# Branch 0's merge products in pairs by seven block products, sums and mix on GpSimd, engine orders by slot

## The chip, the core and the metric

One NeuronCore of a Trainium2 chip runs the whole block in one launch. It has five engines with instruction queues of their own: TensorE (PE, matmuls into PSUM; PEld in the profile is its weight load), VectorE (DVE), ScalarE (ACT), GpSimd (POOL) and SyncE (SP, which issues all DMAs here). They run in parallel and wait for each other through semaphores. The metric is the device time of one execution in microseconds, of which the median over several runs counts; a profile shows one execution.

## The reference

A transformer block of width 1024 over 512 tokens (and 16 meta tokens in front): one input projection `proj = rmsnorm(h) @ w_in`, latent attention (branch 0, MLA) and attention with a forget gate (branch 1, FoX), then the merge:

```python
y_mla = (o_mla * jax.nn.silu(z_mla)) @ w_br_mla[l]
...
y_fox = (o_fox * jax.nn.silu(z_fox)) @ w_br_fox[l]
mixed = (jax.nn.sigmoid(gate_a) * y_mla + jax.nn.sigmoid(gate_b) * y_fox) @ w_out[l]
h = h + rmsnorm(mixed, post_norm_g[l])
```

All of it is f32. `gate_a` and `gate_b` are columns of `proj`. The change is in these four lines: the products with `w_br_mla` (1024 x 1024 weights, 512 tokens), the sum of the two gated branches, and the start of the product with `w_out`.

## The kernel before

Every f32 operand of a matmul is split into a high and a low part in a 4-byte matmul format (`wh`, `wl` for weights, `gh`, `gl` for activations): ScalarE casts the high part, VectorE or GpSimd subtracts it from the f32 value (`split_lo`, L104). A product is then three passes, high x high, high x low, low x high. Activations lie transposed, 128 features on the partitions, tokens along the row.

TensorE's order is written out by hand over the whole kernel; on the other engines a scheduler places instructions by priority, and a few are pinned. Weights come by DMA into one of three buffers `wraw` (512 KB each, `wload`, L106), and are split into one of three pairs `wh`/`wl`. Up to the end of the attention, GpSimd makes the low parts of weights; behind it `low[0]` is VectorE, and GpSimd has nothing more to do.

The merge (from L1062):

- A **gate unit** (`gate_unit`, L534; PSUM tile `pg`) computes 128 columns of `gate_a` or `gate_b` from the block's input in 24 matmuls of 512 tokens, and ScalarE puts the tanh of it into a tile `th`. Eleven of the 16 gates fall into the merge.
- **Branch 1** (`pair_py`, L1130) treats the 1024 x 1024 product as a 2 x 2 block matrix of 512, and the tokens as two halves of 256, and forms it by seven block products in place of eight. A pair of output blocks, `i` and `i + 4`, is one unit: seven products of 12 matmuls with 256 tokens, into PSUM tiles `x`, `y`, `z`. For that the weight blocks (`b11`, `b12`, `b21`, `b22`, in `wraw`) are combined by four sums (`comb`, L1128, VectorE) and seven of them are split (`take`, L1141, ScalarE and VectorE); the activation blocks are combined once (`S1` to `S4`). Products shared by several outputs are copied from PSUM by ScalarE (L1171, L1174, L1178), and VectorE adds and multiplies with the gate (`gated`, L1158, two instructions L1160 and L1161).
- **Branch 0** (`py`, L1083) takes the plain way: eight units of 24 matmuls with 512 tokens (PSUM tile `py`), a gate product on VectorE (L1088), the sum with branch 1's result (L1092, VectorE), and the split of the sum for the output product (L1094, L104).
- **The output product** also goes by seven block products, over `wout` blocks held in four tiles `tb0` to `tb3`, which `tsum` (L1097, VectorE) combines, and over sums of the mixed activations that `ssum` (L1104, VectorE) makes; their splits go to `a1`, `a2` and parts of `uTh`, `uTl`.

Of the kernel before, what the change touches and what calls it, by code (L numbers as in the profile page):

```python
# [23 lines left out]
S = 512  # L24
# [31 lines left out]
def block_kernel(ctx: ExitStack, tc: tile.TileContext, x, meta_tokens, pre_norm_g, w_in, fox_forget_b,  # L56
# [474 lines left out]
    gates = [(i, br) for br in (1, 0) for i in PAIRED]  # L531
# [530 lines left out]
    with ExitStack() as mg:  # L1062
# [15 lines left out]
        def halved_g(br):  # L1078
            for k in range(KD):
                nc.scalar.copy(gh[:, k], gT[br][:, k])  # L1080
                split_lo(nc.vector, gl[:, k], gT[br][:, k], gh[:, k])

        def py(i, br):  # L1083
            def get():
                return by_k(wunit([wbr[br][:, :, 128 * i : 128 * i + 128]])[0], KD)

            def done(_, ps):
                nc.vector.scalar_tensor_tensor(out=gT[br][:, i], in0=ths[i, br], scalar=1.0, in1=ps, op0=ALU.add, op1=ALU.mult)  # L1088
            run(unit(f"py{i}{br}", get, lambda k: (gh[:, k, :], gl[:, k, :]), KD, [slice(0, S)], done))
            if br:  # L1090
                return
            nc.vector.tensor_tensor(out=mx[:, i], in0=mx[:, i], in1=gT[1][:, i], op=ALU.add)  # L1092
            src, (h, l) = (mx[:, i, 0:256], [t[:, i] for t in a1]) if i < HK else (mx[:, i], [t[:, i - HK] for t in a2])
            nc.scalar.copy(h, src)  # L1094
            split_lo(nc.vector, l, src, h)

        def tsum(n, half):  # L1097

            ks = slice(2 * half, 2 * half + 2)
            t11, t12, t22, t21 = (t[:, ks] for t in tb)  # L1100
            out, a, b = ((t11, t12, t11), (t12, t22, t12), (t22, t22, t11), (t21, t21, t22))[n]
            nc.vector.tensor_tensor(out=out, in0=a, in1=b, op=ALU.subtract)

        def ssum(ks):  # L1104

            kt = slice(ks.start + HK, ks.stop + HK)
            m11, m21, m12, m22 = mx[:, ks, 0:256], mx[:, ks, 256:512], mx[:, kt, 0:256], mx[:, kt, 256:512]
            for o, p, q, op in ((m22, m21, m22, ALU.add), (m21, m11, m21, ALU.subtract), (m11, m22, m11, ALU.subtract),
                                (m12, m12, m11, ALU.subtract)):
                nc.vector.tensor_tensor(out=o, in0=p, in1=q, op=op)  # L1110
            for x, h, l in zip((m22, m11, m21, m12), sh, sl):
                nc.scalar.copy(h[:, ks], x)
                split_lo(nc.vector, l[:, ks], x, h[:, ks])

        lo_, up = slice(0, 256), slice(256, 512)
        kb = [slice(0, HK), slice(HK, KD)]

        def split_to(to, src):
            nc.scalar.copy(to[0], src)  # L1119
            split_lo(nc.vector, to[1], src, to[0])  # L1120

        A11, A12, A22, S1 = ([t[:, kb[q], ts] for t in (gh, gl)] for q, ts in ((0, lo_), (1, lo_), (1, up), (0, up)))
        S2, S3, S4 = a1, [t[:, :, lo_] for t in a2], [t[:, :, up] for t in a2]

        g11, g21, g12, g22 = (gT[1][:, kb[q], ts] for q, ts in ((0, lo_), (0, up), (1, lo_), (1, up)))

        def comb(out, p, q, op=ALU.subtract):
            nc.vector.tensor_tensor(out=out, in0=p, in1=q, op=op)  # L1128

        def pair_py(i, br):  # L1130

            j, g, wb = i + HK, gT[br], wbr[br]
            ra, rb = (wload([wb[:, :, 128 * f : 128 * f + 128]])[1] for f in (i, j))
            yield
            b11, b21, b12, b22 = ra[:, 0:512], ra[:, 512:], rb[:, 0:512], rb[:, 512:]
            X, Y, Z = (sp.tile([128, 512], F32, tag="s", name=f"{n}{i}{br}")[:, 0:256] for n in "xyz")
            c11, c21, c12, c22 = g[:, i, lo_], g[:, i, up], g[:, j, lo_], g[:, j, up]
            th1, th2 = ths[i, br], ths[j, br]
            room = []

            def take(src):  # L1141
                if not room:
                    uid[0] += 1
                    hl = [wp.tile([128, 1024], F32R, tag=t, name=f"{t}{uid[0]}") for t in ("wh", "wl")]
                    room.extend([[t[:, sl] for t in hl] for sl in (slice(0, 512), slice(512, 1024))])
                to = room.pop(0)
                split_to(to, src)
                return to

            def prod(ps, a, w, first, last):  # L1150
                q = 0
                for k in range(HK):
                    for wx, ax in ((w[0], a[0]), (w[0], a[1]), (w[1], a[0])):
                        mm(ps, wx[:, 128 * k : 128 * k + 128], ax[:, k], start=(first and q == 0), stop=(last and q == 11),
                           skip_group_check=True)
                        q += 1

            def gated(dst, th, ts, ps, add):  # L1158
                if add:
                    held[:] = [nc.vector.tensor_tensor(out=dst, in0=ps, in1=dst, op=ALU.add).ins]  # L1160
                return nc.vector.scalar_tensor_tensor(out=dst, in0=th[:, ts], scalar=1.0, in1=dst if add else ps, op0=ALU.add, op1=ALU.mult)  # L1161

            w11 = take(b11)
            comb(b11, b12, b11)
            t1 = take(b11)
            yield
            comb(b12, b22, b12)
            comb(b11, b22, b11)
            t2 = take(b11)
            prod(X, A11, w11, True, False)  # L1170
            nc.scalar.copy(c11, X)  # L1171
            w21 = take(b21)
            prod(Z, S1, t1, True, False)
            nc.scalar.copy(c22, Z)  # L1174
            t3 = take(b12)
            comb(b21, b21, b11)
            prod(X, S2, t2, False, False)
            nc.scalar.copy(c12, X)  # L1178
            w22 = take(b22)
            prod(Y, A12, w21, True, True)  # L1180
            gated(c11, th1, lo_, Y, True)
            t4 = take(b21)
            prod(X, S3, t3, False, False)
            gated(c22, th2, up, X, True)
            read = held[0]
            prod(Z, S4, w22, False, True)
            gated(c12, th2, lo_, Z, True)
            held[:] = [read]
            prod(X, A22, t4, False, True)
            closed[i] = gated(c21, th1, up, X, False).ins  # L1190

        closed = {}
        pairs = [pair_py(i, 1) for i in range(HK)]
        with tc.issue_after(normed[0]):
            split_to(A11, g11)
            split_to(A22, g22)
            comb(g22, g21, g22, ALU.add)
            split_to(S1, g22)
        run(gate_unit())
        next(pairs[0])  # L1200
        with tc.issue_after(normed[0]):
            comb(g21, g11, g21)
            comb(g11, g22, g11)
            split_to(S2, g11)
        next(pairs[0])
        run(gate_unit())
        with tc.issue_after(normed[0]):
            split_to(A12, g12)
            comb(g12, g12, g11)
            split_to(S3, g21)  # L1210
            split_to(S4, g12)
        for i in range(HK):
            for _ in pairs[i]:
                pass
            for half in range(2):
                run(gate_unit())
                held.clear()
            if i == 0:
                for n, (q, c) in enumerate(((0, 0), (0, 1), (1, 1), (1, 0))):
                    for half in range(2):  # L1220
                        k0 = HK * q + 2 * half
                        nc.sync.dma_start(tb[n][:, 2 * half : 2 * half + 2], wout[:, k0 : k0 + 2, 512 * c : 512 * c + 512])
            with tc.issue_after(closed[i]):
                for n in ((), (0,), (1,), (2, 3))[i]:
                    for half in range(2):
                        tsum(n, half)
        halved_g(0)
        for n, i in enumerate(PAIRED):
            py(i, 0)
            if gates:  # L1230
                run(gate_unit())
            elif n >= 4:
                done = n // 2 if n < 7 else HK
                if n in (4, 5, 7):
                    ssum(slice({4: 0, 5: 2, 7: 3}[n], {4: 2, 5: 3, 7: 4}[n]))

        nc.scalar.activation(eps_t[0:1, 0:1], ths[PAIRED[-1], 0][0:1, 0:1], AF.Square)
        nc.scalar.activation(eps_t[0:1, 0:1], eps_t[0:1, 0:1], AF.Sqrt)


        mgg.close()
# [20 lines left out]
        def put_in(n, c, to):  # L1262
            raw = tb[n][:, 2 * c : 2 * c + 2]
            hi, lo = (t.rearrange("p k s -> p (k s)").rearrange("p (k f) -> p k f", k=2) for t in to)
            nc.scalar.copy(hi, raw)
            split_lo(nc.vector, lo, raw, hi)
# [39 lines left out]
        X, Z = ([op5.tile([128, 512], F32, tag="po", name=f"{n}{r}") for r in range(2)] for n in "xz")  # L1306
        Y = [acc(f"y{r}") for r in range(2)]
        s_ = list(zip(sh, sl))
        product(X, a1, 0, lambda c: plain(0, 0, c), True, False)
        for r in range(2):  # L1310
            nc.scalar.copy(yo[:, r, N0], X[r])
# [82 lines left out]
```

## Time and profile before

| | us |
|---|---|
| median of 3 runs | 587.23 |
| lowest, highest run | 587.06, 587.66 |
| span of the profiled execution (first to last instruction) | 584.6 |
| first matmul of branch 1's pairs | 408.61 |
| first matmul of branch 0's products | 491.56 |
| first matmul of the output product | 540.52 |

The page gives the busy time of each engine and, as "the chain that ended last", what released what, from the last instruction back. A busy engine is not the bound by itself; the chain and the waits tell that. In rows by group, `out<-in` names tiles, then come the shapes (partitions x elements), the count, busy time and mean duration, and idle time ahead with what ended it.

### The profile page before, as it was taken

How to read it: one execution, taken by the hardware profiler on the slowest of the kernel's cores; microseconds unless marked ns; L12 is line 12 of the kernel's file. 1: busy time of each engine (PE TensorE's matmuls, PEld its weight loads, DVE VectorE, ACT ScalarE, POOL GpSimd, SP SyncE). 2: the span in 40 equal slices, each digit the busy share in tenths (PEclk: the TensorE clock that was granted, in tenths of full speed). 3: DMA queues.
4: the chain of work that ended last, by engine and by line, in shares of the span. 5: the costliest groups of instructions: out<-in, count | busy, mean ns of one | idle time of the engine just before them, and what ended most of it. 6: DMA issues, size and time to landing. Idle time of an engine off the chain costs nothing.

```text
span 584.6 us, 11115 instructions
## 1 busy us (share of the span) xinstructions
PE 575.7 (98%) x3841; PEld 496.8 (85%) x3841; DVE 416.4 (71%) x1156; ACT 357.4 (61%) x816; POOL 199.4 (34%) x270
## 2 busy tenths in 40 slices
PE   8999999999999999999999999999999999999996
PEld 6989889889889888888898898878998998888884
DVE  5854877885776775767758748896647876468966
ACT  7856774893774775767748747944343462443762
POOL 4317745464468462654554634510000000000000
PEclk9999999999999999999999999999999999999998
DMA  8535599989977999988986976977722534233503
GB/s 295 122 83 163 127 176 230 231 195 248 177 167 158 228 191 206 219 172 207 183 176 180 219 154 147 183 172 236 233 73 72 145 104 144 78 109 108 217 0 144
DMA packets 220000, 97.47 MB, mean 167 GB/s; under 512 B 131456, under 2 KB 209672, under 8 KB 219944
## 3 DMA queue, kind: packets, MB, share of 16 engines
q1 hardware_dynamic: 219944, 96.77, 70.3%
q8 instruction: 30, 0.49, 0.3%
q14 instruction: 26, 0.21, 0.1%
HBM read 62.36 MB, written 3.97 MB: 113 GB/s over the span
## 4 chain that ended last, share of the span: by engine, by line
PE 96%; ACT 1%; DMA 1%; issue 0%; SPq 0%; DVE 0%; POOL 0%; DVEq 0%; ACTq 0%; POOLq 0%
PE z L98 19%; PE pg L98 15%; PE v L98 9%; PE fk L98 8%; PE st L98 8%; PE fq L98 8%; PE x L98 8%; PE py L98 7%; PE ov L98 5%; PE psm L98 3%; PE y L98 2%; PE mq L98 2%; PE mk L98 1%; PE ppe L98 1%; DMA wsr<-in_w_in_dram 1%; ACT uTh L371 0%
## 5 line engine op out<-in xcount | busy, mean ns | idle before, releaser
L104 POOL TENSOR_TENSOR wl<-wraw,wh 128x1024 fp32r<-128x1024 f32 (+2 forms) x61 | 118.3, 1947 | 112.2 <-ACT wh L131 80.5
L131 ACT CAST wh<-wraw 128x1024 fp32r<-128x1024 f32 (+1 forms) x72 | 74.6, 1042 | 56.4 <-PE py L98 16.8
L826 ACT ACTIVATE sf<-sf,nb 128x272 f32<-128x272 f32 (+3 forms) x128 | 72.7, 569 | 11.5 <-DVE nb L791 10.6
L865 DVE SCALAR_TENSOR_TENSOR pn<-sf,ri,pn 128x512 f16<-128x512 f32 (+3 forms) x128 | 69.6, 609 | 1.6 <-ACT pn L861 1.5
L104 DVE TENSOR_TENSOR wl<-wraw,wh 128x512 fp32r<-128x512 f32 (+1 forms) x55 | 52.2, 950 | 23.9 <-ACT wh L1119 17.8
L861 ACT ACTIVATE pn<-sf,ri 128x128 f16<-128x128 f32 (+3 forms) x128 | 59.7, 548 | 0.5 <-DVE ri L831 0.5
L98 PE MATMUL z<-uTh,wh 128*128 128x512 f32 x128 | 50.9, 398 | 0.0
L98 PE MATMUL pg<-uTh,wh 128*128 128x512 f32 x128 | 50.2, 392 | 0.0
L98 PE MATMUL z<-uTl,wh 128*128 128x512 f32 x128 | 50.1, 391 | 0.0
L98 PE MATMUL z<-uTh,wl 128*128 128x512 f32 x128 | 50.0, 390 | 0.0
L98 PE MATMUL pg<-uTl,wh 128*128 128x512 f32 x128 | 49.9, 390 | 0.0
L98 PE MATMUL pg<-uTh,wl 128*128 128x512 f32 x128 | 49.8, 389 | 0.0
L706 DVE TENSOR_REDUCE vsc<-v 128x1 f32<-128x272 f32 (+1 forms) x32 | 13.2, 433 | 39.8 <-PE v L98 39.8
L98 PE MATMUL st<-hlk,hlq 64*128 64x272 f32 (+4 forms) x480 | 41.3, 299 | 0.0
L1119 ACT CAST wh<-wraw 128x512 fp32r<-128x512 f32 x28 | 17.3, 618 | 37.9 <-DVE wraw L1128 17.0
L98 PE MATMUL v<-uTh,wl 128*128 128x256 f32 (+1 forms) x128 | 36.5, 285 | 0.0
L98 PE MATMUL fk<-uTl,wh 128*128 128x256 f32 (+1 forms) x128 | 36.4, 285 | 0.0
L98 PEld LDWEIGHTS st<-hlk,hlq 64*128 64x128 f32 x480 | 33.0, 186 | 4.1 <-ACT vh L725 2.8
L98 PE MATMUL fk<-uTh,wh 128*128 128x256 f32 (+1 forms) x128 | 36.4, 285 | 0.0
L98 PE MATMUL v<-uTl,wh 128*128 128x256 f32 (+1 forms) x128 | 36.4, 285 | 0.0
L98 PE MATMUL fk<-uTh,wl 128*128 128x256 f32 (+1 forms) x128 | 36.4, 285 | 0.0
L98 PE MATMUL v<-uTh,wh 128*128 128x256 f32 (+1 forms) x128 | 36.4, 284 | 0.0
(295 smaller groups left out, 1612.3 us busy)
## 6 DMA issues: line engine op xcount, KB each, us to landing
wraw<-in_w_in_dram SPq DMA_DIRECT2D x56, 512.0 KB, 4.8
cbp<-c_dram SPq DMA_DIRECT2D x16, 264.0 KB, 4.1
wraw<-in_w_br_fox_dram SPq DMA_DIRECT2D x8, 512.0 KB, 4.5
tb<-in_w_out_dram SPq DMA_DIRECT2D x8, 512.0 KB, 5.4
wraw<-in_w_br_mla_dram SPq DMA_DIRECT2D x8, 512.0 KB, 4.3
wraw<-in_w_out_dram SPq DMA_DIRECT2D x6, 512.0 KB, 3.6
xr<-in_x_dram SPq DMA_DIRECT2D x4, 512.0 KB
out_dram<-yo SPq DMA_DIRECT2D x8, 256.0 KB, 2.0
```

Of the source, the lines that this page charges most:

```text
L98: nc.tensor.matmul(*a, **k)
L104: return eng.tensor_tensor(out=lo, in0=src, in1=f32(hi), op=ALU.subtract)
L131: nc.scalar.copy(wh[:, :n], raw[:, :n])
L706: nc.vector.tensor_reduce(out=sc[:, i : i + 1], in_=ps, op=ALU.max, axis=AX.X, apply_absolute_value=True)
L826: exps[b // 3] = nc.scalar.activation(sf, sf, AF.Exp, bias=sums["nb"][:, h, b : b + 1], scale=-1.0, accum_out=sums["su"][:, h, b : b + 1]).ins
L861: normed[:] = [nc.scalar.activation(hi, sf, AF.Copy, scale=rib).ins]
L865: nc.vector.scalar_tensor_tensor(out=lo, in0=sf, scalar=rib, in1=hi, op0=ALU.mult, op1=ALU.subtract)
L1119: nc.scalar.copy(to[0], src)
```

## The change

Branch 0's weights go by the same pairs of seven block products as branch 1's: `add_pair(i, br)` takes the place of `pair_py` and `py`, for both branches. Weight sums (`tcomb`), most activation sums, `tsum`, `ssum` and the sum of the branches (`mixed`) are put on GpSimd (`EP`). The first split of the mixed activations (`a1`, three of four blocks), most of the `ssum` splits, that of `a2`'s upper half and one half of the last `tb3` split go to GpSimd too, cast and difference. Branch 0's gates come in another order, and gate units stand 1, 1, 1, 2 behind branch 1's pairs and 2, 1, 1, 0 behind branch 0's (before: two behind each branch-1 pair, one behind branch 0's first unit).

The order on ScalarE, VectorE and GpSimd is no longer left to the scheduler: TensorE's work of the merge is a list `slots` (one block product, or a quarter of a gate, each), and `at(n, fn)` notes what the others get just ahead of slot `n`; `play` writes it all out in this order. Loads stand 8 and 6 slots ahead of a pair.

```diff
+        EV, EP = nc.vector, nc.gpsimd
+        def split_to(to, src, eng=None):
+            (eng.tensor_copy if eng else nc.scalar.copy)(to[0], src)
+            return split_lo(eng or nc.vector, to[1], src, to[0]).ins
+        def comb(eng, out, p, op, q):
+            eng.tensor_tensor(out=out, in0=p, in1=q, op=ALU.add if op == "+" else ALU.subtract)
         def tsum(n, half):
...
-            nc.vector.tensor_tensor(out=out, in0=a, in1=b, op=ALU.subtract)
+            comb(EP, out, a, "-", b)
...
+        def at(n, fn, *a):
+            aux.setdefault(n, []).append(lambda: fn(*a))
+        def add_gate():
...
+            at(n - 8, lambda: getattr(st["g"][0][1], "load")())
+            at(n - 2, lambda: st["g"][0][1].prep())
+            for q in range(4):
+                slots.append(lambda q=q: run(st["g"][2 * q : 2 * q + 2]))
+        def add_pair(i, br):
...
+            def mixed(f, ts):
+                if not br:
+                    comb(EP, mx[:, f, ts], mx[:, f, ts], "+", gT[1][:, f, ts])
+            at(n - 8, load, j, "b12", "b22")
+            at(n - 6, load, i, "b11", "b21")
+            at(n - 4, tcomb, "b12", "b22", "-", "b12")
+            at(n - 3, take, "w11", "b11")
+            at(n - 2, tcomb, "b11", "b12", "+", "b11")
+            at(n - 2, take, "w21", "b21")
+            at(n - 1, take, "t2", "b11")
+            at(n - 1, tcomb, "b21", "b21", "-", "b11")
+            at(n, banks)
+            at(n, tcomb, "b11", "b22", "-", "b11")
+            at(n + 1, evict, c11, "X")
+            at(n + 1, take, "t1", "b11")
+            at(n + 2, gated, c11, "t1", lo_, "Y", True)
+            at(n + 2, take, "t3", "b12")
...
+            for ps, a, key, first, last in (("X", A11, "w11", True, False), ("Y", A12, "w21", True, True),
+                                            ("X", S2, "t2", False, False), ("Z", S1, "t1", True, False),
+                                            ("X", S3, "t3", False, False), ("Z", S4, "w22", False, True),
+                                            ("X", A22, "t4", False, True)):
+                slots.append(lambda *p, a=(ps, a, key, first, last): prod(*a))
...
         for i in range(HK):
+            n = add_pair(i, 1)
+            for _ in range((1, 1, 1, 2)[i]):
+                add_gate()
...
+            if i in (1, 2):
+                at(n + (3, 1)[i - 1], tsum, i - 1, 0)
+                at(n + (5, 3)[i - 1], tsum, i - 1, 1)
+            if i == 2:
+                at(n + 5, comb, EP, h21, h21, "+", h22)
...
+        for i in range(HK):
+            n = add_pair(i, 0)
+            for _ in range((2, 1, 1, 0)[i]):
+                add_gate()
+            if i == 0:
+                for q in range(4):
+                    at(n + (1, 3, 5, 8)[q], tsum, 2 + q // 2, q % 2)
...
+        region.enter_context(tc.manual_schedule(engines={mybir.EngineType.Activation, mybir.EngineType.DVE, mybir.EngineType.Pool}))
+        def play(first, last):
+            for n in range(first, last):
...
+                    for fn in aux.get(n, []):
+                        fn()
+                if 0 <= n < len(slots):
+                    slots[n]()
...
+        at(end + 4, early[1], EP)
+        at(end + 5, early2[1], EP)
+        at(end + 5, last[1], EP)
+        for q in (3, 2):
+            for fs in (early, early2, last):
+                at(end + 6, fs[q], EP)
+        at(end + 7, blocks, S4, HK, up, slice(0, HK), EP)
+        at(end + 7, lambda: w4.append(put_in(3, 0, a1)))
```

**First piece: pair 2 of branch 1.** VectorE before, in its whole order: `wraw74` and `wraw75` hold the pair's weight blocks, `wl76` to `wl79` are the low parts that its products read, L1128 are the weight sums, L1102 `tsum`, L1160 and L1161 the gate instructions.

```order
L104 TENSOR_TENSOR wl76_5957<-wraw74_5949,wh76_5956 128x512
L1128 TENSOR_TENSOR wraw74_5949<-wraw75_5951,wraw74_5949 128x512
L1128 TENSOR_TENSOR wraw75_5951<-wraw75_5951 128x512
L104 TENSOR_TENSOR wl76_5957<-wraw74_5949,wh76_5956 128x512
L1128 TENSOR_TENSOR wraw74_5949<-wraw75_5951,wraw74_5949 128x512
L104 TENSOR_TENSOR wl77_5966<-wraw74_5949,wh77_5965 128x512
L1128 TENSOR_TENSOR wraw74_5949<-wraw74_5949 128x512
L104 TENSOR_TENSOR wl77_5966<-wraw74_5949,wh77_5965 128x512
L104 TENSOR_TENSOR wl78_5998<-wraw75_5951,wh78_5997 128x512 x2
L104 TENSOR_TENSOR wl79_6032<-wraw74_5949,wh79_6031 128x512
```

VectorE in the changed kernel at the same place; the pair's low parts are now `wl74`, `wl75`, `wl77` and `wl79`, and L1196 and L1197 are the gate instructions.

```order
L104 TENSOR_TENSOR wl74_5871<-wraw73_5833,wh74_5870 128x512 x2
L104 TENSOR_TENSOR wl75_5890<-wraw73_5833,wh75_5889 128x512 x2
L1196 TENSOR_TENSOR gT1_779<-y21_5905,gT1_779 128x256
L1197 SCALAR_TENSOR_TENSOR gT1_779<-th21_5435,gT1_779 128x256
L104 TENSOR_TENSOR wl77_5939<-wraw71_5795,wh77_5938 128x512 x2
L104 TENSOR_TENSOR wl79_5974<-wraw73_5833,wh79_5973 128x512
```

GpSimd in the changed kernel there (before it had no instruction in the merge): the weight sums (L1087) of `wraw71` and `wraw73`, the two halves of `tb1`, and the first sum of branch 0's activations `gT0`.

```order
L1087 TENSOR_TENSOR wraw73_5833<-wraw71_5795,wraw73_5833 128x512
L1087 TENSOR_TENSOR wraw73_5833<-wraw73_5833 128x512
L1087 TENSOR_TENSOR wraw73_5833<-wraw71_5795,wraw73_5833 128x512
L1087 TENSOR_TENSOR tb1_5462<-tb2_5463,tb1_5462 128x1024 x2
L1087 TENSOR_TENSOR gT0_778<-gT0_778 128x4x256
```

The four weight sums and the two halves of `tb1` have moved from VectorE to GpSimd, one after another there, and a sum of `gT0` is new behind them; the splits have stayed on VectorE, each behind a cast of what GpSimd has summed.

**Second piece: branch 0's first products.** VectorE before, from the first `py`: whole weight tiles are split, a gate product (L1088) and the sum of the branches (L1092) stand between them.

```order
L104 TENSOR_TENSOR wl91_6395<-wraw91_6392,wh91_6394 128x1024
L104 TENSOR_TENSOR wl92_6428<-wraw92_6425,wh92_6427 128x1024
L1088 SCALAR_TENSOR_TENSOR gT0_778<-th00_5744,py000_6363 128x512
L1092 TENSOR_TENSOR gT0_778<-gT0_778,gT1_779 128x512
L104 TENSOR_TENSOR wl93_6463<-wraw93_6460,wh93_6462 128x1024
```

VectorE in the changed kernel, from the activation splits for branch 0's pairs to the last weight split of its first pair.

```order
L104 TENSOR_TENSOR wl89_6240<-wraw88_6213,wh89_6239 128x512
L104 TENSOR_TENSOR a2l_5468<-gT0_778,a2h_5467 128x4x256
L104 TENSOR_TENSOR wl89_6240<-wraw88_6213,wh89_6239 128x512
L104 TENSOR_TENSOR wl90_6261<-wraw88_6213,wh90_6260 128x512
L104 TENSOR_TENSOR gl_5454<-gT0_778,gh_5453 128x4x256
L104 TENSOR_TENSOR wl90_6261<-wraw88_6213,wh90_6260 128x512
L1196 TENSOR_TENSOR gT0_778<-y00_6278,gT0_778 128x256
L1197 SCALAR_TENSOR_TENSOR gT0_778<-th00_5902,gT0_778 128x256
L104 TENSOR_TENSOR wl92_6312<-wraw87_6191,wh92_6311 128x512 x2
L104 TENSOR_TENSOR wl94_6347<-wraw88_6213,wh94_6346 128x512
```

GpSimd there: the weight sums of this pair and the two halves of `tb2`.

```order
L1087 TENSOR_TENSOR wraw87_6191<-wraw87_6191 128x512
L1087 TENSOR_TENSOR wraw88_6213<-wraw87_6191,wraw88_6213 128x512
L1087 TENSOR_TENSOR wraw88_6213<-wraw88_6213 128x512
L1087 TENSOR_TENSOR wraw88_6213<-wraw87_6191,wraw88_6213 128x512
L1087 TENSOR_TENSOR tb2_5463<-tb2_5463,tb0_5461 128x1024 x2
```

Where one whole-tile split stood for each `py`, seven half-tile splits stand for each pair, and behind four of them lies a sum on GpSimd; `tb2` and `tb3` fall into this pair.

**Third piece: the end of GpSimd's order in the changed kernel**, during the output product (casts L1083, differences L104; before, ScalarE and VectorE made all of these).

```order
L1083 CAST uTh_68<-gT1_779 128x256
L104 TENSOR_TENSOR uTl_69<-gT1_779,uTh_68 128x256
L1083 CAST a2h_5467<-gT0_778 128x4x256
L104 TENSOR_TENSOR a2l_5468<-gT0_778,a2h_5467 128x4x256
L1083 CAST a1h_5465<-tb3_5464 128x1024
L104 TENSOR_TENSOR a1l_5466<-tb3_5464,a1h_5465 128x1024
```

The last two rows make half of the weights that the last four blocks of the output product read.

282 lines of the change are left out of this document (153 added, 129 removed).

## Prediction, made before the changed kernel was run

> **What bounds the kernel now.** First the page: busy time by engine, and the chain that ended last.
>
> ```profile
> PE 575.7 (98%) x3841; PEld 496.8 (85%) x3841; DVE 416.4 (71%) x1156; ACT 357.4 (61%) x816; POOL 199.4 (34%) x270
> ...
> PE 96%; ACT 1%; DMA 1%; issue 0%; SPq 0%; DVE 0%; POOL 0%; DVEq 0%; ACTq 0%; POOLq 0%
> ```
>
> TensorE is the bound, and nothing that it waits for stands in the chain. Whatever shortens its work shortens the run, as long as the others still deliver in time. Next the chain in order of time through the merge (start, length, what):
>
> ```profile
> 408.61 1.43 PE x L98 x12
> 410.04 1.44 PE z L98 x12
> 411.48 1.38 PE x L98 x12
> 412.86 1.42 PE y L98 x12
> 414.28 1.38 PE x L98 x12
> 415.66 1.36 PE z L98 x12
> 417.02 1.42 PE x L98 x12
> 418.44 10.91 PE pg L98 x48
> ...
> 491.56 5.44 PE py L98 x24
> 497.00 5.44 PE pg L98 x24
> 502.44 38.08 PE py L98 x168
> 540.52 5.49 PE x L98 x24
> ```
>
> One pair of branch 1 is 9.83 us (the seven rows of 12), two gates are 10.91, a branch-0 unit `py` and a single gate 5.44, an output product 5.44 to 5.49; no row waits. Who works beside it, by stage (length, PE, PEld, DVE, ACT, POOL busy, then the granted clock):
>
> ```profile
> core 0: us, PE busy (x) PEld busy (x) DVE busy (x) ACT busy (x) POOL busy (x), PEclk, DMA share, GB/s
> ...
> 408.40:491.50 83.10, 83.10 (x530) 75.49 (x530) 60.27 (x90) 36.71 (x63) 0.00 (x0) 1.00 0.42 122
> 491.50:540.50 49.00, 49.00 (x218) 40.59 (x217) 30.89 (x46) 19.55 (x30) 0.00 (x0) 1.00 0.39 118
> 540.50:584.60 44.10, 38.31 (x169) 31.22 (x167) 34.33 (x53) 23.98 (x43) 0.00 (x0) 0.96 0.30 120
> ```
>
> GpSimd does nothing at all in the last 176 us; VectorE has slack in each stage. The change fills GpSimd.
>
> **What it saves.** Eight `py` of 5.44 become four pairs of 9.83: 43.5 - 39.3 = **4.2 us** of TensorE. The gates and the output products keep their number. If all else hid, the time would be 587.2 - 4.2 = 583.0.
>
> **What the moved work costs.** Behind row 408 GpSimd gets 97 instructions (15 two-operand ones of 1024 elements, 39 of 512, 30 of 256, one of 768, 12 casts), where it had none. VectorE loses its sums and keeps every split that feeds TensorE. Durations:
>
> ```profile
> L104 POOL TENSOR_TENSOR wl<-wraw,wh 128x256 fp32r<-128x256 f32 x16 | 11.5, 739 | 31.7 <-ACT wh L607 25.8 <-DMA qpe_dram<-gT 5.9
> ...
> L666 POOL TENSOR_TENSOR gT<-gT 128x512 f32<-128x512 f32 x2 | 2.6, 1289 | 2.9 <-DVE gT L659 2.9
> ```
>
> ```profile
> L104 DVE TENSOR_TENSOR wl<-wraw,wh 128x1024 fp32r<-128x1024 f32 x25 | 30.4, 1219 | 6.1 <-ACT wh L131 6.0
> L104 DVE TENSOR_TENSOR wl<-wraw,wh 128x512 fp32r<-128x512 f32 x28 | 19.3, 690 | 17.8 <-ACT wh L1119 17.8
> ...
> L1161 DVE SCALAR_TENSOR_TENSOR gT<-th,gT 128x256 f32<-128x256 f32 x12 | 5.1, 423 | 0.3
> ```
>
> So GpSimd takes 0.74 for 256 and 1.29 for 512 elements, VectorE 0.42, 0.69 and 1.22 for 256, 512 and 1024. Whether the two run side by side, the trace shows at few places. VectorE's rows, then GpSimd's, at the start of the merge and at 93 us:
>
> ```profile
> 379.83 2.35 DVE L104 TENSOR_TENSOR gl<-gT,gh 128x1024 fp32r<-128x1024 f32 x2
> 382.21 3.31 DVE L1128 TENSOR_TENSOR gT<-gT 128x1024 f32<-128x1024 f32 x1
> 385.45 1.21 DVE L104 TENSOR_TENSOR gl<-gT,gh 128x1024 fp32r<-128x1024 f32 x1
> ```
>
> ```profile
> 381.53 2.91 POOL L104 TENSOR_TENSOR wl<-wraw,wh 128x1024 fp32r<-128x1024 f32 x1 [3.36 <-ACT wh L131]
> ```
>
> ```profile
> 93.56 0.68 DVE L104 TENSOR_TENSOR hlq<-fq,hlq 128x512 fp32r<-128x512 f32 x1
> ```
>
> ```profile
> 93.54 2.40 POOL L104 TENSOR_TENSOR wl<-wraw,wh 128x1024 fp32r<-128x1024 f32 x1 [1.65 <-ACT wh L131]
> ```
>
> At 93 us VectorE reads one operand from PSUM (`fq`) and both keep their usual time: 0.68, and 2.40 for GpSimd's 1024. At 382 both of VectorE's operands lie in SBUF, and the two take **turns**. GpSimd's row begins at 381.53, VectorE's second split ends at 382.18, and from there GpSimd needs 2.26, to 384.44. VectorE's sum begins at 382.21, takes 3.31 instead of 1.21 and ends at 385.52, 1.08 behind GpSimd's end. Each waits for the whole of the other's instruction, first come first served, and all that runs beside the other is about 0.14 at an instruction's start.
>
> A rule decides how far that reaches. The Trainium skill has two: "Advanced Engine Details and Errata" (VectorE Performance Modes) names only VectorE's two-port modes as those that block GpSimd; "SBUF — State Buffer" (Who interferes with whom) adds every VectorE instruction with two SBUF inputs against a GpSimd one that reads SBUF. By the first, sums of two f32 operands would not wait and the time would be 583.0; by the second it is the sum below. The 3.31 agrees with the second.
>
> Now the turns by stage. Given are TensorE's time; the instructions on the port by elements; their whole durations (GpSimd 2.40, 1.29, 0.74; VectorE 1.22, 0.69, 0.42); the same with 0.14 off each, the least that turns can take; and the stage laid out.
>
> | stage | PE | GpSimd 1024/512/256 | VectorE 1024/512/256 | whole | held | laid out |
> |---|---|---|---|---|---|---|
> | br. 1 pair 0 + gate | 15.3 | 0/5/0 | 1/8/3 | 14.4 | 12.1 | 15.8 |
> | pair 1 + gate | 15.3 | 2/4/0 | 1/7/3 | 17.3 | 14.8 | 18.1 |
> | pair 2 + gate | 15.3 | 3/4/0 | 1/7/3 | 19.7 | 17.1 | 20.2 |
> | pair 3 + 2 gates | 20.7 | 3/3/0 | 8/7/3 | 26.9 | 23.6 | 25.0 |
> | br. 0 pair 0 + 2 gates | 20.7 | 4/5/4 | 3/7/3 | 28.8 | 25.1 | 29.4 |
> | pair 1 + gate | 15.3 | 0/4/4 | 1/7/3 | 15.4 | 12.7 | 15.3 |
> | pair 2 + gate | 15.3 | 0/8/4 | 1/7/3 | 20.6 | 17.3 | 18.0 |
> | pair 3 | 9.8 | 0/0/6, a cast and a difference of 768 | 1/4/3 | 12.4 | 10.1 | 11.2 |
> | first two output products | 10.9 | 0/4/10 | 4/3/4, one of 768 | 20.0 | 16.5 | 15.2 |
> | the rest | 27.2 | 4/2/8 | 7/11/0 | 29.7 | 25.3 | 32.7 |
>
> A cast on GpSimd counts with its tile size: 0.61 for 512, about 1.1 for 1024.
>
> ```profile
> L668 POOL CAST gT<-pt 128x512 fp32r<-128x512 f32 x2 | 1.2, 610 | 0.0
> ```
>
> "Laid out" means the rows of the four engines in their written order under one another, each beginning when the one ahead on its engine is through, when its data are there and when the port is free. Pair 2 of branch 1 shows how (the order's first piece): GpSimd has its last weight sum, both halves of `tb1` and the 4x256 sum of `gT0` in a row, 1.29 + 3 x 2.40 = 8.5. Between two of them VectorE gets one turn: the last split of `wl75`, a gate product, the first split of `wl77`. The first `wl77` split, which the fifth of the seven products reads, comes through 2.9 instead of 0.69 after it was asked for. TensorE waits 1.0 for `wl75` and 4.0 for `wl77`: 4.9 in this stage. Branch 0's first pair loses 8.7 in the same way (two halves each of `tb2` and `tb3` among its splits; the second piece). At the end the splits of `a2` and of `a1` from `tb3`, last of GpSimd's 12 pairs of cast and difference (third piece), keep the last products waiting 4.6. Laid out with hand-overs left out, the sum moves by less than 2.5.
>
> Over TensorE's time that is 0.5 + 2.8 + 4.9 + 4.3 + 8.7 + 0 + 2.7 + 1.4 + 4.3 + 5.5 = **35.1**. By whole durations it is 40, by held parts 17.0 (where a stage holds less than TensorE's time, 0). I take 35: the orders are strict, and a split that has lost its turn keeps what stands behind it waiting while the port is idle. Laying out the program of before in this way gives the last matmul within 0.3 of its row.
>
> Edits at nothing: ScalarE's evictions and casts (it was busy for 36.71 of 83.10 and 19.55 of 49.00); the weight loads, issued six to eight blocks ahead, over 8 us at 1.4 a block, against
>
> ```profile
> wraw<-in_w_br_mla_dram SPq DMA_DIRECT2D x8, 512.0 KB, 4.3
> ```
>
> and the new order of gates, since each `th` is made before its pair. That VectorE loses its sums gains nothing by itself, since it was not on the chain.
>
> **Sum.** The profiled execution's span is 584.6, 2.6 under the median of 587.2; both have the same work, so I add to the median: 587.2 - 4.2 + 35.1 = 618.
>
> **Rivals.**
> *No turns*: the long row at 382 was a special case, and GpSimd's work hides. Laid out without the port, TensorE waits under half a microsecond in all: **583.0**, faster. For it: GpSimd idle now, VectorE with slack, one such sum row only. Against: three numbers of that place (2.91, 3.31, and 1.08 behind the end) fit turns to a few hundredths. It decides from where GpSimd's rows block for half of what they show: then the 35 falls to 3, less than the 4.2 saved.
> *Turns at their least*: the waits among the stages even out and only held parts count: 587.2 - 4.2 + 17.0 = **600**. Against it: the strict order on three engines.
> *The clock falls*: behind the last matmul TensorE stands idle, and the granted clock follows:
>
> ```profile
> 578.80:581.30 2.50, 0.01 (x1) 0.00 (x0) 1.98 (x5) 0.98 (x3) 0.00 (x0) 1.00 0.55 213
> 581.30:584.60 3.30, 0.00 (x0) 0.00 (x0) 0.48 (x1) 0.00 (x0) 0.00 (x0) 0.51 0.41 159
> ```
>
> 2.5 us of idleness and it is half. Two waits of the layout reach 3 to 4 us (pair 2, the last product). If each has the next 3 us at half speed, 1.5 is lost twice: **621**. The Trainium skill ("TensorE: Matmul & The Clock Gate", What's actually happening) gives windows of about 3.4 us for both ways; by that it would be an estimated 1.7 each.
> *Whole durations in every stage*: 587.2 - 4.2 + 40 = **623**.
> That fewer products run isn't in doubt: the rows of TensorE change from 24 of 512 a unit to 84 of 256 a pair.
>
> **Chances.** Forecast 0.58, clock or whole durations 0.20, least turns 0.13, no turns 0.07, a mix near no change 0.02. Within 0.2% (1.2 us) is what a measurement can't tell from no change: faster 0.07, same 0.02, slower 0.91. The range goes from the least turns to 623 with the clock's loss and a little for GpSimd's spread, 600 to 627; it leaves out 583 and what lies around it.
>
> **What would show it.** GpSimd's 1024 rows above 2.8 and VectorE's 512 splits above 1.2 in pair 2 and in branch 0's first pair, and VectorE's rows with a PSUM operand unchanged at 0.42; TensorE waiting there for `wl` from VectorE, and at the end for `a1l` from GpSimd; a pair without waits at 9.8. Wrong would be: VectorE's splits at 0.69 beside GpSimd's rows (then 583), or TensorE waiting for loads.

## The result, and the profile after

| | before | changed |
|---|---|---|
| median | 587.14 us (4 runs) | 623.45 us (4 runs) |
| lowest, highest | 586.97, 587.66 | 622.63, 624.95 |
| span of the profiled execution | 584.6 | 620.8 |

The changed kernel is slower by a factor of 1.0622 (95% interval 1.0607 to 1.0638), 36.3 us where 31 were forecast. From the page of the changed kernel: busy time of the engines, the clock granted to TensorE by fortieths of the span, and the chain that ended last, by engine.

```profile
PE 587.9 (95%) x3985; PEld 508.9 (82%) x3985; DVE 443.1 (71%) x1136; ACT 362.7 (58%) x833; POOL 348.1 (56%) x367
...
PEclk9999999999999999999999999999989889998997
...
PE 70%; POOL 10%; DVE 8%; ACT 4%; issue 4%; DMA 3%; POOLq 0%; DVEq 0%; ACTq 0%
```

Before, the chain was 96% TensorE, with GpSimd at 0%. Now GpSimd and VectorE hold 18% of it. VectorE has 20 instructions fewer and is busy 26.7 us longer (443.1 against 416.4): its instructions have become longer. What TensorE waits for, by releaser (us in total, times, the longest):

```profile
PE x L98 <- DVE wl L104: 8.4, 6, 3.6
PE z L98 <- DVE wl L104: 5.8, 6, 1.7
PE pg L98 <- DVE wl L104: 3.2, 2, 2.1
PE x L98 <- DVE pad L1378: 3.0, 1, 3.0
PE x L98 <- DVE gT L1196: 2.1, 2, 1.6
```

Pair 2 of branch 1, the first place of the prediction, in the changed kernel's timeline: VectorE, GpSimd, then the matmul that waits (start, length, what). L1087 are the sums now, L1196 and L1197 the gate instructions.

```profile
446.31 2.21 DVE L104 TENSOR_TENSOR wl<-wraw,wh 128x512 fp32r<-128x512 f32 x1 [2.13 <-ACT wh L1083]
448.44 0.41 DVE L1196 TENSOR_TENSOR gT<-y,gT 128x256 f32<-128x256 f32 x1
448.89 2.15 DVE L1197 SCALAR_TENSOR_TENSOR gT<-th,gT 128x256 f32<-128x256 f32 x1
450.97 4.03 DVE L104 TENSOR_TENSOR wl<-wraw,wh 128x512 fp32r<-128x512 f32 x3
```

```profile
445.57 5.19 POOL L1087 TENSOR_TENSOR tb<-tb,tb 128x1024 f32<-128x1024 f32 x2
450.72 2.52 POOL L1087 TENSOR_TENSOR gT<-gT 128x1024 f32<-128x1024 f32 x1
```

```profile
453.85 0.39 PE L98 MATMUL x<-a2h,wl 128*128 128x256 f32 x1 [3.58 <-DVE wl L104]
```

One split of 512 takes 2.21 in place of 0.69, a gate product of 256 takes 2.15 in place of 0.42, and the next split again starts behind a GpSimd sum, the one that begins at 450.72. Between two long rows stands one of 0.41: it reads `y`, which lies in PSUM, and it runs inside the row of GpSimd that lasts until 450.76. TensorE waits 3.58 for the split.

Stage by stage, from the first matmul of each in the timeline of the changed kernel. "Over" is the length less TensorE's own time (15.3, 20.7 and so on, as in the prediction's table; 27.0 in the last row, which ends where its last matmul starts).

| stage | first matmul at | length | over | laid out |
|---|---|---|---|---|
| br. 1 pair 0 + gate | 408.18 | 15.6 | 0.3 | 0.5 |
| pair 1 + gate | 423.79 | 19.0 | 3.7 | 2.8 |
| pair 2 + gate | 442.80 | 22.2 | 6.9 | 4.9 |
| pair 3 + 2 gates | 464.95 | 26.5 | 5.7 | 4.3 |
| br. 0 pair 0 + 2 gates | 491.40 | 28.0 | 7.3 | 8.7 |
| pair 1 + gate | 519.43 | 15.3 | 0.0 | 0.0 |
| pair 2 + gate | 534.73 | 18.4 | 3.1 | 2.7 |
| pair 3 | 553.16 | 11.4 | 1.6 | 1.4 |
| first two output products | 564.59 | 15.1 | 4.2 | 4.3 |
| the rest, to the last matmul at 614.15 | 579.65 | 34.5 | 7.5 | 5.5 |
| sum | | | 40.3 | 35.1 |

40.3 less the 4.2 saved is 36.1, which is the measured difference within 0.2. No stage is off by more than 2.0. The three that exceed their forecast most (pairs 2 and 3 of branch 1 by 2.0 and 1.4, the last row by 2.0) had a granted clock of 0.92, 0.94 and 0.90. But the clock doesn't order the stages by itself: branch 0's first pair (0.94) and the first two output products (0.89) came out below their forecast, and pair 1 of branch 1 is 0.9 above it at full clock. TensorE's rows by windows of the changed kernel (length, busy times, and the granted clock behind POOL's column):

```profile
core 0: us, PE busy (x) PEld busy (x) DVE busy (x) ACT busy (x) POOL busy (x), PEclk, DMA share, GB/s
447.00:456.00 9.00, 4.29 (x29) 3.88 (x29) 8.30 (x7) 2.73 (x5) 6.24 (x3) 0.93 0.03 8
456.00:460.00 4.00, 4.00 (x26) 3.91 (x25) 3.39 (x6) 0.16 (x1) 1.29 (x1) 0.73 1.07 310
485.00:489.50 4.50, 4.50 (x14) 3.55 (x13) 4.50 (x2) 1.56 (x2) 4.06 (x2) 0.62 0.46 117
498.00:504.00 6.00, 4.27 (x23) 3.98 (x24) 5.96 (x6) 2.44 (x5) 5.64 (x4) 0.72 0.00 0
567.00:571.00 4.00, 3.72 (x9) 2.95 (x10) 3.96 (x7) 1.69 (x3) 2.83 (x3) 0.57 0.65 167
605.00:612.00 7.00, 6.12 (x14) 4.46 (x15) 5.21 (x9) 1.64 (x5) 2.02 (x1) 0.52 0.29 112
```

Busy time times the missing share of the clock gives 0.3 + 1.1 + 1.7 + 1.2 + 1.6 + 2.9 = an estimated 8.8 us for the five places (the first two rows are one place). The other 31 or so are waits and the restarts behind them.

### The profile page after: what moved, and what is told of

The parts are those of the page before. It is cut to its first block, busy times and chain, and to the rows that moved or that the text cites. A ratio compares the mean times of both kernels' runs of the same rounds, so it can differ in the third digit from the quotient of the medians.

```text
span 620.8 us, 11543 instructions
## 1 busy us (share of the span) xinstructions
PE 587.9 (95%) x3985; PEld 508.9 (82%) x3985; DVE 443.1 (71%) x1136; ACT 362.7 (58%) x833; POOL 348.1 (56%) x367
## 4 chain that ended last, share of the span: by engine, by line
PE 70%; POOL 10%; DVE 8%; ACT 4%; issue 4%; DMA 3%; POOLq 0%; DVEq 0%; ACTq 0%
PE z L98 16%; PE v L98 8%; PE fk L98 8%; PE pg L98 8%; PE st L98 7%; PE fq L98 7%; DVE wl L104 6%; PE ov L98 5%; POOL wraw L1087 3%; PE x L98 3%; PE psm L98 2%; POOL gT L1087 2%; POOL uTl L104 2%; ACT wh L1083 2%; PE mq L98 2%
## 5 line engine op out<-in xcount | busy, mean ns | idle before, releaser
L104 POOL TENSOR_TENSOR wl<-wraw,wh 128x1024 fp32r<-128x1024 f32 (+2 forms) x61 | 117.7, 1937 | 110.9 <-ACT wh L131 74.3
L104 DVE TENSOR_TENSOR wl<-wraw,wh 128x512 fp32r<-128x512 f32 (+1 forms) x74 | 81.6, 1122 | 51.7 <-ACT wh L1083 45.8
L131 ACT CAST wh<-wraw 128x1024 fp32r<-128x1024 f32 (+1 forms) x63 | 65.1, 1039 | 30.6 <-PE v L98 10.0
L1083 ACT CAST wh<-wraw 128x512 fp32r<-128x512 f32 x56 | 33.3, 620 | 56.9 <-POOL wraw L1087 27.1
```

The costliest lines, as they stand in the source:

```text
L104: return eng.tensor_tensor(out=lo, in0=src, in1=f32(hi), op=ALU.subtract)
L131: nc.scalar.copy(wh[:, :n], raw[:, :n])
L1083: (eng.tensor_copy if eng else nc.scalar.copy)(to[0], src)
```

## The experiments

**GpSimd writes, but reads nothing.** If the turns are the cause, they have to go when GpSimd stays as busy at the same places and only stops reading SBUF. In the changed kernel every GpSimd sum of the merge (and cast and difference of the tail) becomes memsets of about its length:

```diff
+        def blank(out, reads, n):
+            for x in reads:
+                nc.gpsimd.memset(x[tuple(slice(0, 1) if k else slice(None) for k in range(len(x.shape)))], 0.5)
+            for _ in range(n):
+                nc.gpsimd.memset(f32(out), 0.5)
+            half = out.shape[-1] // 2
+            if n == 2 and int(np.prod(out.shape)) > 128 * 256:
+                nc.gpsimd.memset(f32(out[..., :half]), 0.5)
...
         def comb(eng, out, p, op, q):
+            if eng is nc.gpsimd:
+                return blank(out, [p, q], 2)
```

> Each GpSimd sum, cast and difference of the merge is replaced by memsets of the same output tile that take about as long (two whole ones and a half one for 2.40 or 1.29, two for 0.74), and a one-column memset of each input, which keeps the waits on what makes the inputs. GpSimd then writes SBUF but reads none. These sums and splits are left out, so the merge's numbers are others. Turns on reading: no VectorE split waits, the 512 splits of wl stay at 0.69 beside GpSimd's memsets, TensorE's waits fall under 1 us each, and the laid-out orders without the port give 589 (587 to 592). Rival, GpSimd is just slow and stands at a bad place in the order: its rows are as long and stand where they stood, so TensorE waits as before, 615 to 623. Rival, turns on writing too: as slow as the changed kernel, 618 to 624.

Measured: 597.85 us, 1.0173 of before (1.0150 to 1.0195); 25.6 less than the changed kernel, but not 589. The turns are gone: VectorE's splits of 512 in the merge take 689 ns. The waits of TensorE that are left come from the experiment itself, as the next run bears out. GpSimd and TensorE in pair 1 of branch 1:

```profile
427.85 0.10 POOL L1084 MEMSET wraw<- 128x1 f32 x1 [1.40 <-DVE wl L104]
```

```profile
431.67 0.39 PE L98 MATMUL z<-gh,wh 128*128 128x256 f32 x1 [0.76 <-ACT wh L1095]
```

A memset of a column in an input that an earlier split still reads has to wait for that split, here 1.40; a sum only reads the input, as the split does, and needn't wait. So this kernel was run again without these columns for weight sums and `wout` sums:

```diff
-                return blank(out, [p, q], 2)
+                return blank(out, [x for x in (p, q) if x.tensor.name.startswith('gT')], 2)
```

> The first memset kernel waited 10.9 more than the kernel before, at the product with S1 in each pair, and the trace puts it down to my one-column memsets: the one on the shared input of two weight sums had to wait for VectorE's split to have read it, which a sum doesn't. Here those columns are left out for weight sums and wout sums, so that GpSimd's memsets are as long as its sums and wait only for what a sum waits for on its output. Left out are the same sums and tail splits as in the first. Turns on reading, and nothing else: the orders laid out without the port give 583 (582 to 588), faster than before. Rival, part of the loss comes from GpSimd's place and length in the order: it stays near the first, 594 to 600. Rival, the clock: no stretch below 0.95 is left, so nothing there.

Measured: **584.94 us, 0.9967 of before (0.9954 to 0.9980)**. Its page, VectorE's splits of 512 and 1024 in the merge, and GpSimd's memsets of the same tiles as the `tb` sums (two of them and a half one, 0.53, per sum):

```profile
PE 573.4 (99%) x3985; PEld 501.3 (86%) x3985; DVE 392.4 (67%) x1136; ACT 362.9 (62%) x833; POOL 315.2 (54%) x585
```

```profile
L104 DVE TENSOR_TENSOR wl<-wraw,wh 128x512 fp32r<-128x512 f32 x54 | 36.4, 690 | 51.2 <-ACT wh L1095 51.2
L104 DVE TENSOR_TENSOR wl<-wraw,wh 128x1024 fp32r<-128x1024 f32 x14 | 17.1, 1221 | 2.0 <-ACT wh L131 1.9
```

```profile
L1086 POOL MEMSET tb<- 128x1024 f32 x16 | 15.3, 956 | 0.5
```

The same 54 splits in the changed kernel:

```profile
L104 DVE TENSOR_TENSOR wl<-wraw,wh 128x512 fp32r<-128x512 f32 x54 | 55.9, 1060 | 46.0 <-ACT wh L1083 45.8
```

With 54% busy GpSimd, VectorE's rows are back at 690 and 1221 ns, and TensorE's busy time falls by 14.5 (587.9 to 573.4) for the same 3985 matmuls, the slow clock among it. The list of TensorE's waits has 0.2 left in the merge:

```profile
PE z L98 <- DVE wl L104: 0.2, 1, 0.2
```

GpSimd instructions of about the sums' length, in the sums' place in the order, cost nothing as long as they don't read. What they leave out besides the reading is the wait for a weight that a sum reads but doesn't overwrite. The run also bears out that the seven products save time, 2.2 of the 4.2 that were counted.

**The same turns without the change.** Does it need shared tiles, or semaphores between the two engines? The kernel before gets GpSimd work in the merge that nobody waits for, on a scratch tile of its own:

```diff
+        scr = m1.tile([128, 256], BF16, tag="scr", name="scr")
+        nc.gpsimd.memset(scr, 0.0)
+        nc.gpsimd.tensor_copy(scr[:, 0:1], g22[:, 0, 0:1])
+        for n in range(80):
+            nc.gpsimd.tensor_tensor(out=scr, in0=scr, in1=scr, op=ALU.subtract)
```

> The kernel before, with 80 GpSimd instructions added in the merge that nobody waits for: each subtracts a scratch tile of 128x256 bf16 from itself (about 0.74 by the f32 row of that size), from about 397 on. The outputs are not touched. Turns: VectorE's splits that begin beside one are up to 0.6 longer than 0.69 and 1.22, GpSimd's rows up to 1.1 longer, and VectorE's rows with a PSUM operand stay at 0.42. The time stays within 0.5 of before (laid out +0.3), because each turn is short and the splits of this kernel are made well ahead. Rival, no turns for a scratch tile that VectorE never touches (the long rows come from shared tiles or from semaphores): 0.69 and 1.22 unchanged. Rival, every turn costs: 80 turns of about 0.6 on VectorE would bring 10 us or more.

And its counterpart:

```diff
-        for n in range(80):
-            nc.gpsimd.tensor_tensor(out=scr, in0=scr, in1=scr, op=ALU.subtract)
+        for n in range(160):
+            nc.gpsimd.memset(scr, 0.0)
```

> As the kernel with dummy reads, but with 160 memsets of the same 128x256 bf16 tile (0.32 each by the row of that size) in place of the 80 subtractions. Turns on reading: VectorE's splits keep 0.69 and 1.22 and the time stays at 587. Rival, turns on any GpSimd access: splits up to 0.3 longer.

Measured with reads: 589.88, 1.0046 of before (1.0029 to 1.0062); with writes: 586.70, 0.9992 (0.9982 to 1.0002). VectorE by groups between 397 and 480, and GpSimd's group, with reads:

```profile
L104 DVE TENSOR_TENSOR wl<-wraw,wh 128x512 fp32r<-128x512 f32 x26 | 26.7, 1047 | 5.3 <-ACT wh L1119 5.2
...
L1160 DVE TENSOR_TENSOR gT<-y,gT 128x256 f32<-128x256 f32 x3 | 1.3, 425 | 3.0 <-PE y L98 3.0
```

```profile
L1216 POOL TENSOR_TENSOR scr<-scr 128x256 bf16<-128x256 bf16 x80 | 76.0, 950 | 6.3
```

The same, with writes:

```profile
L104 DVE TENSOR_TENSOR wl<-wraw,wh 128x512 fp32r<-128x512 f32 x26 | 17.9, 690 | 17.9 <-ACT wh L1119 17.9
```

```profile
L1216 POOL MEMSET scr<- 128x256 bf16 x160 | 49.9, 312 | 9.2
```

A tile that VectorE never touches makes its splits 1047 long instead of 690, and the row that reads PSUM keeps 425. So it is the reading that takes turns, and neither the data nor a semaphore. It needn't be a sum of two tiles: GpSimd's casts, which read one, take turns too. Two of the same size in the changed kernel, the first beside a split of VectorE, the second beside a row with a PSUM operand:

```profile
594.35 1.39 POOL L1083 CAST uTh<-gT 128x256 fp32r<-128x256 f32 x1
```

```profile
597.37 0.39 POOL L1083 CAST uTh<-gT 128x256 fp32r<-128x256 f32 x1
```

The price of the dummy reads was underrated: 2.8 in place of 0.3. Most of it is one wait, at the end of the stretch, where VectorE had used up its lead (busy for 22.2 of the 22.4 us up to there; with reads):

```profile
PE x L98 <- DVE gT L1160: 2.3, 1, 2.3
```

**Which part costs.** First all of it back on VectorE and ScalarE, in the slot orders of the changed kernel:

```diff
-        EV, EP = nc.vector, nc.gpsimd
+        EV, EP = nc.vector, nc.vector
...
-        at(end + 4, early[1], EP)
+        at(end + 4, early[1])
```

(and so for the other tail splits).

> The changed kernel with its slot orders as they are, but all sums and the mix on VectorE, and the twelve tail splits on ScalarE (cast) and VectorE (difference): GpSimd is idle in the merge again. Turns: no VectorE row of the merge beside a GpSimd one, 512 splits at 0.69; what is left is that VectorE's strict order now holds the sums too, laid out 597 (594 to 600). Rival, the written slot orders are what costs, whichever engine has the sums: 612 or more. Rival, the seven products themselves are slower than counted (84 of 256 take 9.83 only in branch 1): 605 or more, and pairs of branch 0 above 9.83 without a wait.

Then the sums and the mix alone, with the tail splits left on GpSimd:

```diff
-        EV, EP = nc.vector, nc.gpsimd
+        EV, EP, EG = nc.vector, nc.vector, nc.gpsimd
...
-        at(end + 4, early[1], EP)
+        at(end + 4, early[1], EG)
```

> Only the sums and the mix go back to VectorE; the twelve tail pairs of cast and difference (S2 of a1, most of the ssum splits, S4 of a2, half of tb3) stay on GpSimd. Turns, laid out: stages of the pairs without long rows, the tail still held up by GpSimd's casts and differences, 600 (597 to 604). Without turns the same layout gives 590. Rival, the tail is where most of the loss lies: 612 or more.

And the tail splits alone, with the sums left on GpSimd:

```diff
-                at(n + 4, blocks, S2, 0, lo_, slice(0, 3), EP)
+                at(n + 4, blocks, S2, 0, lo_, slice(0, 3))
...
-        at(end + 4, early[1], EP)
+        at(end + 4, early[1])
```

> Only the twelve tail pairs go back to ScalarE and VectorE; the sums and the mix stay on GpSimd. Turns, laid out: the pairs lose what they lost, the tail gains little because the losses ahead of it stay, 617 (613 to 622). Without turns the layout gives 589. Rival, the tail splits on GpSimd are the main loss: 600 or less.

| sums and mix | tail splits | median | of before |
|---|---|---|---|
| GpSimd | GpSimd (the changed kernel) | 623.45 | 1.0622 (1.0607 to 1.0638) |
| GpSimd | VectorE | 623.69 | 1.0620 (1.0601 to 1.0639) |
| VectorE | GpSimd | 602.35 | 1.0249 (1.0223 to 1.0274) |
| VectorE | VectorE | 601.12 | 1.0231 (1.0214 to 1.0249) |

The sums are worth 21 to 23 us, the tail splits nothing that these runs can tell. Both runs with VectorE's splits lie above their forecast and outside its range, 601 against 597 and 624 against 617; the third, 602 against 600, lies within. In the two that miss it, TensorE loses most in one place of the tail: the third output product (`z`) takes 11.8 and 14.4 us from its first matmul to the next product's, in place of 5.44. In the kernel with all on VectorE:

```profile
560.51 0.80 PE L98 MATMUL z<-wh,uTh 128*128 128x512 f32 x1 [2.67 <-ACT wh L131]
561.10 0.63 PE L98 MATMUL z<-wh,uTl 128*128 128x512 f32 x1
564.35 0.79 PE L98 MATMUL z<-wl,uTh 128*128 128x512 f32 x1 [2.62 <-DVE wl L104]
```

Behind two waits of 2.6 the rows that take 0.39 elsewhere take 0.63, which is the slow clock (0.58 granted between 560.5 and 572.3). So the rival of the slot orders was right in part: with no turn left, the written orders, with the sums on VectorE, still lose 14 us against before. In the kernel with the sums on GpSimd and the tail splits on VectorE, one wait at the same product is longer still, which is why moving the splits gained nothing:

```profile
586.28 0.79 PE L98 MATMUL z<-wl,uTh 128*128 128x512 f32 x1 [5.71 <-DVE wl L104]
```

**A version that beats both, and the same with GpSimd.** What is left is the order. Starting from the kernel with all on VectorE, the written order of ScalarE, VectorE and GpSimd goes, the seven products (and with them the sums and splits of a pair) get the order they have in the kernel before, the `tb` sums, the activation sums behind branch 1 and the gates' splits are queued behind VectorE's read of `x`, one gate moves from branch 0's first pair to branch 1's last, and the splits of `ssum` stand behind the output products that don't read them:

```diff
-        region.enter_context(tc.manual_schedule(engines={mybir.EngineType.Activation, mybir.EngineType.DVE, mybir.EngineType.Pool}))
...
+        def late(fn, *a):
+            with tc.issue_after(held[0]):
+                fn(*a)
...
+                    read = nc.vector.tensor_tensor(out=dst, in0=r[ps], in1=dst, op=ALU.add).ins
+                    if ps == "X":
+                        held[:] = [read]
...
-            for ps, a, key, first, last in (("X", A11, "w11", True, False), ("Y", A12, "w21", True, True),
-                                            ("X", S2, "t2", False, False), ("Z", S1, "t1", True, False),
+            for ps, a, key, first, last in (("X", A11, "w11", True, False), ("Z", S1, "t1", True, False),
+                                            ("X", S2, "t2", False, False), ("Y", A12, "w21", True, True),
...
-            for _ in range((1, 1, 1, 2)[i]):
+            for _ in range((1, 1, 1, 3)[i]):
...
-            for _ in range((2, 1, 1, 0)[i]):
+            for _ in range((1, 1, 1, 0)[i]):
```

> A version that may beat both: branch 0 by seven products as in the changed kernel, all sums, the mix and all splits off GpSimd, the seven products of a pair in the order of the kernel before (x z x y x z x), the written order of ScalarE, VectorE and GpSimd replaced by the scheduler with VectorE's reads of x ahead of later sums and splits, gates 1, 1, 1, 3 and 1, 1, 1, 0, and the splits of the output product's sums behind the products that don't need them. Turns as the main loss: laid out 584.2, so 583 to 588, with waits of TensorE under 1 us each. Rival, VectorE has no room for the sums of four more pairs: 590 or more, with waits for wl all through branch 0.

Measured: **583.98 us, 0.9949 of before (0.9935 to 0.9962)**, with the whole computation in it. Its page (engines, and the chain that ended last):

```profile
PE 573.0 (98%) x3985; PEld 500.7 (86%) x3985; DVE 442.8 (76%) x1221; ACT 369.9 (64%) x845; POOL 199.6 (34%) x270
...
PE 96%; ACT 1%; DMA 1%; issue 0%; SPq 0%; DVE 0%; POOL 0%; DVEq 0%; ACTq 0%; POOLq 0%
```

VectorE is as busy as in the changed kernel (442.8 against 443.1) and TensorE waits for nothing in the merge. One name was then changed back:

```diff
-        EV, EP = nc.vector, nc.vector
+        EV, EP = nc.vector, nc.gpsimd
```

> The scheduled version of the run before, with one name changed: the sums and the mix on GpSimd in place of VectorE (the tail splits stay off GpSimd). The scheduler then also orders them. Turns: the sums take turns with the splits and TensorE waits through all pairs, laid out 615 (608 to 624). Without turns this order gives 596. Rival, the written slot orders of the changed kernel were the fault and the scheduler repairs it with GpSimd too: 584 to 590.

Measured: 619.17, 1.0539 of before (1.0520 to 1.0557). Its longest waits, and its splits of 512:

```profile
PE x L98 <- ACT gT L1196: 12.9, 5, 5.6
PE x L98 <- DVE gT L1200: 4.2, 1, 4.2
```

```profile
L104 DVE TENSOR_TENSOR wl<-wraw,wh 128x512 fp32r<-128x512 f32 x54 | 61.6, 1169 | 25.3 <-ACT wh L1083 24.4
```

The engine of the sums alone is worth 35.2 us here. Not all of that is turns: the largest group, 12.9, are waits for ScalarE's copy of `x` out of PSUM, which stands behind casts that wait for GpSimd's weight sums (up to 6.39 at 432). This order was laid out for VectorE, and even without turns 596 was expected for it with the sums on GpSimd. How the 35.2 divide between turns and GpSimd's longer sums was not run by itself.

## Why the prediction was right, point by point

- **4.2 us saved on TensorE: 2 to 3.4 shown.** The second memset kernel and the scheduled one run at 584.94 and 583.98, 2.2 and 3.1 under before in the same comparison. TensorE is busy 2.3 and 2.7 less than before's 575.7, From the first matmul of the pairs to the start of the last matmul, TensorE needs 169.97 before, 167.00 and 166.56 in these two: 3.0 and 3.4 less. A pair of branch 0 without waits takes the 9.83 that was counted (in the changed kernel 519.43 to 529.26). The rest of the 4.2 is not accounted for, but for 0.3 at one halt in the scheduled kernel's second pair of branch 0, which takes 10.14.
- **Turns between VectorE's instructions with two SBUF operands and GpSimd's that read SBUF: shown,** from both sides. Without GpSimd's reads the rows are back at 0.69 and 1.22 and the loss is gone; with reads of a foreign tile in the kernel before they appear, and the row with a PSUM operand keeps its 0.42. Of the two rules that were weighed, this is the second, and by the Trainium skill ("SBUF — State Buffer", Who interferes with whom) a GpSimd instruction that only writes doesn't contend either: the trace agrees, 690 ns beside 160 memsets.
- **The size, 35.1: measured 40.3.** The step that was mis-sized is the layout of the turns, in which TensorE always ran at full clock. The waits that it gave were about right in place and somewhat large (35 against some 31), and the clock, which stood among the rivals with two places and 1.5 each, took an estimated 8.8 at five places. The two partly cancel, and the sum came out 5 short. (The table of stages holds 93 of the 97 GpSimd instructions; three of the others ran ahead of its first stage. This is too little to bear on the 5.)
- **Pair 2 of branch 1, "1.0 for `wl75` and 4.0 for `wl77`": measured 1.13 and 3.58.** Then the clock fell, which makes 6.9 of 4.9.
- **Branch 0's first pair, 8.7: measured 7.3,** with a clock of 0.72 among it.
- **The end: right in size, wrong in its releaser.** The splits of `a2` and `a1` on GpSimd were to keep the last products waiting 4.6. The last four blocks did wait, 3.04 and 0.34. In the changed kernel, TensorE, then VectorE and GpSimd:

```profile
605.55 0.76 PE L98 MATMUL x<-a1h,a2h 128*128 128x512 f32 x1 [3.04 <-DVE pad L1378]
606.11 0.63 PE L98 MATMUL x<-a1h,a2l 128*128 128x512 f32 x1
607.08 0.80 PE L98 MATMUL x<-a1l,a2h 128*128 128x512 f32 x1 [0.34 <-POOL a1l L104]
```

```profile
600.67 4.13 DVE L1380 SCALAR_TENSOR_TENSOR yo<-yo,pad,xr 128x512 f32<-128x512 f32 x2
604.73 0.68 DVE L1442 TENSOR_TENSOR yo<-x,yo 128x512 f32<-128x512 f32 x1
```

```profile
602.76 1.50 POOL L1083 CAST a1h<-tb 128x1024 fp32r<-128x1024 f32 x1
604.34 2.68 POOL L104 TENSOR_TENSOR a1l<-tb,a1h 128x1024 fp32r<-128x1024 f32 x1
```

  `a1h` was there at 604.26. What came last was, as far as the rows tell, VectorE's read of `x` (L1442, to 605.41), which had to clear the PSUM tile; the releaser that the profile names, L1378 on `pad`, is the row behind it, and TensorE doesn't use `pad`. The read stood behind two output rows of 128x512 that took 4.13 beside GpSimd's splits; the same two take 1.42 without turns in the second memset kernel. The prediction had counted VectorE's own rows at the end, but not as the ones that hold TensorE.
- **The tail splits on GpSimd as a loss of 4.6 of their own: not borne out.** They do cost here, by way of VectorE's output rows. But moving them alone to VectorE changed nothing (623.69 against 623.45), since the wait then lies at the `z` product (5.71).
- **What was to be seen:** VectorE's 512 splits above 1.2 at the two places (2.21 and 2.17), PSUM rows unchanged, TensorE waiting for `wl`, a pair without waits at 9.8: all there. GpSimd's 1024 rows were to be above 2.8: they are 2.84 on average in branch 0's first pair, but 2.62 and 2.52 in pair 2. At the end TensorE waited 0.34 for `a1l`, and most of the time for VectorE.
- **Rivals.** No turns (583): refuted for the changed kernel, and 2 us from what the kernel measures once GpSimd stops reading (584.94). Turns at their least (600): refuted, the gaps between turns don't even out. The clock: it was no rival but an addition, and larger than thought. Whole durations (623): nearest to the measured time, but by luck. Its 40 is made of other parts: it has 9.1 for the first two output products and 2.5 for the rest, where 4.2 and 7.5 were measured, and no loss by the clock.

## What to carry to other kernels

Before work goes to an idle GpSimd, look at what it reads and at what runs on VectorE meanwhile: two f32 operands in SBUF on VectorE and one read on GpSimd run one after the other, and GpSimd's 512 elements hold the place for 1.29 where VectorE would have needed 0.69. What GpSimd did beside VectorE for nothing here was to write, or to work next to instructions that take an operand from PSUM. Where the sums stay on VectorE, the order alone, TensorE's included, was worth 17 us here (601.1 to 584.0), on the same engines and with the same work.

## What was not expected of the hardware

- The granted clock fell to half behind waits much shorter than the prediction's 3 to 4 us: after one of 2.08 (at 484.65, then 0.62 over 4.5 us), and at 498 to 504 around waits of 1.40 and 1.70 (0.72). Two waits of 1.72 and 1.43 in pair 1 were followed by no such stretch, nor was the one of 2.26 in the kernel with dummy reads (granted clock 1.00 in the 7 us behind it). So the length of a wait alone doesn't tell whether the clock falls; what else decides, these runs don't show. The Trainium skill ("TensorE: Matmul & The Clock Gate", What's actually happening) has a window of about 3.4 us that must be idle; the stretches at half clock are near that length (454.7 to 458.0 in pair 2), but an idle time of that length was not needed here.
- 80 short GpSimd reads that nobody waits for made VectorE's splits half as long again, and this moved the time by about half a percent, since these splits are made ahead. The loss in the changed kernel comes from turns in a chain: GpSimd's sum, ScalarE's cast and VectorE's split of the same half tile, each just ahead of its matmul.
